# Attention on one core: the inner sums of V's blocks made by Pool instead of VectorE from the second batch on

## The chip, the cores and the metric

The kernel runs on one core of a Trainium2 chip. The metric is the device time of one execution in microseconds; runs of this kernel are compared by their medians. The core has five engines with instruction streams of their own: TensorE (PE in the profile, with its weight loads as PEld), VectorE (DVE), ScalarE (ACT), Pool (POOL) and SyncE (SP). Pool also issues most of this kernel's loads, so its stream is the queue of the loads as well.

## The reference

For each of 8 batches, with 2048 positions and a width of 512:

```python
scores = np.matmul(q, k.transpose(0, 2, 1)) / np.sqrt(d_k)
attn_weights = special.softmax(scores, axis=-1).astype(np.float32)
return np.matmul(attn_weights, v)
```

All three inputs and the output are float32 of 8 x 2048 x 512.

## The kernel before, in words

Both matrix products are made by a scheme that replaces the eight block products of a 2 x 2 by 2 x 2 product with seven, at the price of sums of blocks ahead of the products and behind them. Operands are float16, sums in PSUM are float32, the exponential is taken without subtracting a maximum, and the row sums of the weights come from a column of ones beside V.

**Scores.** A `Group` (L267 to L331) makes the scores of 1024 queries against 256 keys in seven products on PE (L299); ACT copies and exponentiates (L309, L313, L316, L239), DVE adds two products from PSUM into a buffer `cz` (L319, L322). The sums of K's and Q's blocks are made by DVE (L185 to L188, L202 to L205). The weights go into `left` and `right`.

**Weights times V.** There are 32 groups `g`, four to a batch, each with two blocks `a` and `b` of 256 rows of the output. `Pair` (L471) makes the products 1, 5, 6 and 7 (L512) of each block from the weights, V in `vh` and sums of V's blocks: `vt1`, `vt2` and `vt4`, made by DVE in L219 to L222, word `V` in the order below. The products 2, 3 and 4 of both blocks go through the same scheme once more, in `Leaf` (L402): seven inner products of three parts each (L424, 12 matmuls of 128 x 128), one part for each `h`. The inner V block of `h` = 0 is `vt4`, that of `h` = 1 and 2 the left and right half of the second rows of `vh`. DVE adds each inner product from PSUM into `rows` (L431), ACT scales the rows, and SP stores them.

**The sums that the change touches.** For each `h`, `leaf_v` (L364) cuts the inner V block into four quarters, and `leaf_v_sums` (L372) gives four subtractions on 128 x 512 float16 elements: `t1` and `t2` into buffers `vu` (L376, L377), the third over a quarter of the block itself (L378, it shows as `vh<-vh` or `vt<-vt`), `t4` into `vu` (L379). That is twelve a batch and 96 in all. The inner products read them: 5 reads `t1`, 6 reads `t2`, 7 the third, 4 reads `t4`; 1, 2 and 3 read the block's quarters as they are. There is one set of `vu` buffers for all batches, so a batch's `t1` may be written only when the last inner product 5 of the batch before has read the old one.

**What sets the order.** All engines' streams are written out by hand, as words in `SEQUENCES` (L620), one list for each of the four groups of a batch, with special ones at the start and at the end. Every engine works off its own instructions in that order; waits on semaphores are put in from the data's dependences. A word with a stroke belongs to the group before. The words of the change are `w`, `u` and `n` for `h` = 0, 1 and 2, with the number of the subtraction; `lq`, `lk` and `lv` load a quarter of the next batch's Q, K or V (L131, L211, issued by Pool), and `tq`, `tk` transpose it by a DMA that SP issues (L155). There are two buffers `stage` for the loads of Q and K, so each of these loads waits until the transpose of the load before last has landed. A stretch of the list of a batch's first group reads

```python
"b5 V30 . u0 lq1 . n2 tk0 a7 u1 . xb1 . n1 lv0 . . xa0 xb2 b1 . fa . ha xa1 u3 V31 "
```

The dots are products of the scores, the letters `a` and `b` products of `Pair`. The order is that of the text, but each engine goes through it at its own pace: Pool, which had only loads, ran far ahead of the others.

Of the kernel before, what the change touches and what calls it, by code (L numbers as in the profile page):

```python
# [12 lines left out]
def kernel(  # L13
# [21 lines left out]
    nc = tc.nc  # L35
# [142 lines left out]
    add, sub = nc.vector.tensor_add, nc.vector.tensor_sub  # L178
# [185 lines left out]
    def leaf_v(b, h):  # L364

        w = (vt4[:], vraw[b % 2][:, :, 1, 0:H], vraw[b % 2][:, :, 1, H:])[h]
        t1, t2, t4 = (t[:] for t in vus[h])
        b12 = w[:, 0:NK, Q:H]
        t3 = vraw[(b + 1) % 2][:, 0:NK, 0, h * Q:(h + 1) * Q] if b == B - 1 else b12
        return w[:, 0:NK, 0:Q], b12, w[:, NK:NJ, 0:Q], w[:, NK:NJ, Q:], t1, t2, t3, t4  # L370

    def leaf_v_sums(b, h):  # L372
        b11, b12, b21, b22, t1, t2, t3, t4 = leaf_v(b, h)
        b22, t1 = b22[:, :, 0:Q], t1[:, :, 0:Q]
        return [
            lambda: sub(t1, b12, b11),  # L376
            lambda: sub(t2, b22, t1),  # L377
            lambda: sub(t3, b22, b12),  # L378
            lambda: sub(t4, b21, t2),  # L379
        ]  # L380
# [317 lines left out]
    def step(g, word):  # L698
# [7 lines left out]
        if kind in "abL":  # L706
            pv(g, word)
        elif kind in "Klt":
            next_batch(g, word)
        elif kind == "k":  # L710
            k_sums(int(word[2]))[int(word[1])]()
        elif kind in "xyz":
            weight_sums(g, word)
        elif kind == "v":
            v_sums(g // NQT, int(word[2]))[int(word[1])]()
        elif kind == "V":
            v_sums(g // NQT, 2 * int(word[2]), 2)[int(word[1])]()
        elif kind == "q":
            sp = g // 2 + 1 + g % 2
            if sp < NP // 2:  # L720
                q_sums(sp)[int(word[1])]()
        elif kind in "wun":
            leaf_v_sums(g // NQT, "wun".index(kind))[int(word[1])]()
        elif kind in "fh":
            pairs[g, word[1]].add_right("fh".index(kind) + 1)
        elif kind == "S":
            if leafed(g):
                leaves[g].store(int(word[1]))
        elif kind == "s":
            if leafed(g):  # L730
                leaf_p_sums(g)[int(word[1])]()
# [165 lines left out]
```

## Time and profile before

| | |
|---|---|
| median of 2 runs | 783.42 us (783.31 to 783.54) |
| span of the profiled execution, first to last instruction | 781.0 us |
| what lies around the span, median less span | 2.4 us |
| PE busy | 774.9 us, 99% |
| DVE busy | 744.8 us, 95% |
| ACT busy | 632.4 us, 81% |
| POOL busy | 72.4 us, 9% |

The profile shows one execution. Its page gives the busy time of each engine, the chain of work that ended last, and groups of instructions by source line, with the number of them, the total, the mean of one and the idle time of the engine ahead of them. The trace behind it can be asked for the rows in order of time, for the waits, and for the busy time in chosen stretches. An instruction's duration on DVE reaches a little beyond the start of the next one, so the distance from start to start is shorter than the duration. The granted clock of PE is full (1.00) in all stretches looked at. Times in the text are from the start of the span. The batch shown as the example is the third; its sums lie between 228 and 262 us.

### The profile page before, as it was taken

The page shows a single profiled execution, that of the slowest core. Times are in us where ns is not written, and L with a number is a line of the kernel's source. Part 1 is how long each engine was busy: PE and PEld are TensorE (multiplying, and loading weights), DVE is VectorE, ACT ScalarE, POOL GpSimd, SP SyncE. Part 2 cuts the span into 40 slices and gives each one's busy share as a digit, 9 for nine tenths or more (in the row PEclk, how much of TensorE's full clock was granted, in tenths as well). Part 3 has the DMA queues.
Part 4 walks back from the last instruction along what each step waited for, and adds up shares of the span by engine and source line. Part 5 has one row for each costly group of instructions (what it writes and reads, how often), then busy time and mean ns, then how long its engine had stood idle before and what let it go on. Part 6 is the DMA issues. An engine that isn't in the chain of part 4 may idle for free.

```text
span 781.0 us, 17247 instructions
## 1 busy us (share of the span) xinstructions
PE 774.9 (99%) x6675; PEld 536.7 (69%) x6675; DVE 744.8 (95%) x1466; ACT 632.4 (81%) x1152; POOL 72.4 (9%) x106
## 2 busy tenths in 40 slices
PE   9999999999999999999999999999999999999997
PEld 6566776677766777667676676666776667766687
DVE  6899999999999999999999999999999999999996
ACT  5987888877888778887788877897779977898763
POOL 4011101001010010100100101001010011000000
PEclk9999999999999999999999999999999999999999
DMA  9999777959879696795977969779788995831023
GB/s 224 183 168 157 165 149 152 206 90 167 182 121 193 121 208 143 132 190 114 188 163 138 161 115 182 169 160 136 158 158 149 192 141 136 172 83 55 1 81 136
DMA packets 196386, 115.97 MB, mean 148 GB/s; under 512 B 122448, under 2 KB 187088, under 8 KB 196304
## 3 DMA queue, kind: packets, MB, share of 16 engines
q0 software_dynamic: 49664, 49.29, 41.4%
q1 hardware_dynamic: 145936, 64.73, 35.1%
q8 instruction: 52, 0.85, 0.4%
q10 hardware_dynamic: 704, 0.85, 0.3%
q14 instruction: 30, 0.25, 0.1%
HBM read 100.70 MB, written 33.55 MB: 172 GB/s over the span
## 4 chain that ended last, share of the span: by engine, by line
PE 98%; ACT 1%; DMA 0%; DVE 0%; issue 0%
PE t L299 48%; PE t L512 29%; PE t L424 19%; PE t L259 1%; PE t L165 1%; DMA rows<-in_q_dram 0%; ACT right L239 0%; ACT rows L444 0%; ACT t L309 0%; ACT left L239 0%; PE t L598 0%; ACT cz L316 0%; DVE stage L818 0%; DVE qraw L168 0%; DVE kraw L168 0%
## 5 line engine op out<-in xcount | busy, mean ns | idle before, releaser
L299 PE MATMUL t<-qraw,kraw 128*128 128x512 f16 x744 | 194.2, 379 | 0.0
L512 PEld LDWEIGHTS <-s 128*128 128x128 f16 x1536 | 148.2, 98 | 44.2 <-DVE s L353 0.3
L424 PEld LDWEIGHTS <-right 128*128 128x128 f16 x2232 | 138.1, 97 | 32.0 <-DVE right L397 0.4
L299 PEld LDWEIGHTS <-kraw 128*128 128x128 f16 x1008 | 95.9, 98 | 79.9 <-issue 0.4
L239 ACT ACTIVATE right<-cz 128x1024 f16<-128x1024 f32 x126 | 133.0, 1061 | 14.0 <-DVE cz L319 14.0
L299 PE MATMUL t<-qs,ks 128*128 128x512 f16 x504 | 138.7, 379 | 0.1
L512 PE MATMUL t<-vt,s 128*128 128x256 f16 (+1 forms) x1024 | 132.8, 273 | 0.0
L431 DVE TENSOR_TENSOR rows<-t,rows 128x384 f32<-128x384 f32 x217 | 119.2, 549 | 5.4 <-PE t L424 3.0
L299 PEld LDWEIGHTS <-ks 128*128 128x128 f16 x756 | 71.6, 98 | 58.3 <-issue 1.1
L239 ACT ACTIVATE left<-t 128x512 f16<-128x512 f32 x128 | 77.2, 603 | 25.9 <-PE t L299 23.5
L322 DVE TENSOR_TENSOR cz<-t,cz 128x512 f32<-128x512 f32 x126 | 86.3, 685 | 11.0 <-PE t L299 10.3
L239 ACT ACTIVATE right<-t 128x512 f16<-128x512 f32 x132 | 79.9, 607 | 11.6 <-PE t L299 8.5
L313 ACT COPY cz<-t 128x512 f32<-128x512 f32 x126 | 73.6, 584 | 18.2 <-PE t L299 15.5
L319 DVE TENSOR_TENSOR cz<-t,cz 128x512 f32<-128x512 f32 x126 | 86.0, 682 | 1.5 <-PE t L299 1.3
L444 ACT ACTIVATE rows<-rows,scales 128x512 f32<-128x512 f32 x124 | 83.0, 724 | 0.4 <-DVE rows L431 0.4
L316 ACT COPY cz<-t 128x512 f32<-128x512 f32 x126 | 74.9, 594 | 5.5 <-PE t L299 5.2
L309 ACT COPY t<-t 128x512 f32<-128x512 f32 x123 | 71.0, 577 | 6.8 <-PE t L299 2.0
L424 PE MATMUL t<-vh,right 128*128 128x128 f16 x1004 | 76.4, 218 | 0.0
L299 PE MATMUL t<-qraw,ks 128*128 128x512 f16 x252 | 75.0, 379 | 0.0
L299 PE MATMUL t<-qs,kraw 128*128 128x512 f16 x252 | 74.9, 379 | 0.0
L512 PE MATMUL t<-vh,s 128*128 128x256 f16 x512 | 66.4, 273 | 0.0
L512 PE MATMUL t<-vh,left 128*128 128x256 f16 x512 | 66.3, 273 | 0.0
(90 smaller groups left out, 979.2 us busy)
## 6 DMA issues: line engine op xcount, KB each, us to landing
out_dram<-rows SPq DMA_DIRECT2D x125, 256.0 KB, 2.9
vh<-in_v_dram POOLq DMA_DIRECT2D x32, 512.0 KB, 8.6
stage<-in_q_dram POOLq DMA_DIRECT2D x28, 512.0 KB, 5.9
stage<-in_k_dram POOLq DMA_DIRECT2D x28, 512.0 KB, 5.7
right<-in_k_dram POOLq DMA_DIRECT2D x2, 512.0 KB, 12.6
rows<-in_q_dram SPq DMA_DIRECT2D x2, 256.0 KB, 3.6
cz<-in_q_dram SPq DMA_DIRECT2D x2, 256.0 KB, 4.5
cz<-in_k_dram SPq DMA_DIRECT2D x2, 256.0 KB, 4.4
```

Of the source, the lines that this page charges most:

```text
L165: nc.tensor.transpose(tr[:, m, dc, :], src[:, n + m, dc * P:(dc + 1) * P], ident)
L239: nc.scalar.activation(out=out_, in_=in_, func=EXP, scale=inv_sqrt_d)
L299: nc.tensor.matmul(dst[:], lhs[:, j, dc, :], rhs[:, :, dc, :], start=(n in (1, 5) and dc == 0), stop=(dc == 1), skip_group_check=True,)
L309: self.edges[0](out=self.y[:], in_=self.x[:])
L313: self.edges[1](out=self.cz[:, 0, :], in_=self.z[:])
L316: nc.scalar.copy(out=self.cz[:, 1, :], in_=self.x[:])
L319: nc.vector.tensor_add(self.cz[:, 0, :], self.x[:], self.cz[:, 0, :])
L322: nc.vector.tensor_add(self.cz[:, 1, :], self.z[:], self.cz[:, 1, :])
L424: nc.tensor.matmul(to[:, h * Q:h * Q + w], lhs[:, j, h, :], rhs[:, j, 0:w], start=(n in (1, 2, 5) and h == 0 and j == 0), stop=(j == NK - ...
L431: nc.vector.tensor_add(o, part, o)
L444: nc.scalar.activation(out=o, in_=o, func=COPY, scale=scales[:, g % 2, m, 1 - h:2 - h])
L512: nc.tensor.matmul(dst[:, 0:width], lhs(j), rhs(j), start=(first and j == 0), stop=(j == NJ - 1), skip_group_check=True,)
```

## The change

One line is added to `leaf_v_sums`. For every batch but the first (`b` = 0) the four subtractions are given to Pool; in the first they stay on DVE. That moves 84 instructions from DVE's stream into Pool's. Their words, and so their places in the written order relative to the loads, stay the same.

```diff
@@ -372,6 +372,7 @@
     def leaf_v_sums(b, h):
         b11, b12, b21, b22, t1, t2, t3, t4 = leaf_v(b, h)
         b22, t1 = b22[:, :, 0:Q], t1[:, :, 0:Q]
+        sub = nc.gpsimd.tensor_sub if b else nc.vector.tensor_sub
         return [
             lambda: sub(t1, b12, b11),
             lambda: sub(t2, b22, t1),
             lambda: sub(t3, b22, b12),
             lambda: sub(t4, b21, t2),
         ]
```

Lines from 375 on have a number higher by one after the change.

On Pool, these rows stand in the third batch's first group and the start of its second before the change. `stage` rows are loads of Q and K, `vh` rows are loads of V; the number behind a name tells the buffer.

```order
L131 DMA stage_3126<-in_q_dram 128x4x512
L131 DMA stage_3134<-in_k_dram 128x4x512
L131 DMA stage_3239<-in_q_dram 128x4x512
L211 DMA vh1_94<-in_v_dram 128x4x512
L131 DMA stage_3308<-in_k_dram 128x4x512
L131 DMA stage_3482<-in_k_dram 128x4x512
```

The same place on Pool after the change (the first of the batch's twelve, which writes `vu1_2`, stands right ahead of the first row here):

```order
L131 DMA stage_3126<-in_q_dram 128x4x512
L131 DMA stage_3134<-in_k_dram 128x4x512
L377 TENSOR_TENSOR vu1_1_101<-vh0_93 128x512
L131 DMA stage_3239<-in_q_dram 128x4x512
L379 TENSOR_TENSOR vh0_93<-vh0_93 128x4x128
L378 TENSOR_TENSOR vu2_1_102<-vh0_93,vu1_1_101 128x512
L378 TENSOR_TENSOR vu2_2_105<-vh0_93,vu1_2_104 128x512
L211 DMA vh1_94<-in_v_dram 128x4x512
L380 TENSOR_TENSOR vu4_1_103<-vh0_93,vu2_1_102 128x512
L377 TENSOR_TENSOR vu1_0_98<-vt4_97 128x512
L131 DMA stage_3308<-in_k_dram 128x4x512
L380 TENSOR_TENSOR vu4_2_106<-vh0_93,vu2_2_105 128x512
```

Seven of the batch's twelve subtractions stand in these rows, and four more follow them ahead of the next load. Pool works in this order, so a load that stands behind a subtraction is issued after it, and a subtraction behind a load after that load's wait.

On DVE, these rows stand at the start of the batch's second group before the change. `s`, `left` and `right` are sums of the weights, `rows` and `cz` are fed from PSUM (`t`).

```order
L431 TENSOR_TENSOR rows0_115<-t_3396,rows0_115 128x3x128
L379 TENSOR_TENSOR vu4_2_106<-vh0_93,vu2_2_105 128x512
L397 TENSOR_TENSOR right0_109<-left0_107,right0_109 128x12x128
L378 TENSOR_TENSOR vh0_93<-vh0_93 128x4x128
L378 TENSOR_TENSOR vt4_97<-vt4_97 128x4x128
L377 TENSOR_TENSOR vu2_0_99<-vt4_97,vu1_0_98 128x512
L354 TENSOR_TENSOR s3_114<-left0_107,right0_109 128x1024
```

And the same place on DVE after the change:

```order
L432 TENSOR_TENSOR rows0_115<-t_3396,rows0_115 128x3x128
L398 TENSOR_TENSOR right0_109<-left0_107,right0_109 128x12x128
L354 TENSOR_TENSOR s3_114<-left0_107,right0_109 128x1024
L537 TENSOR_TENSOR rows0_115<-rows0_115 128x256
L322 TENSOR_TENSOR cz_3425<-t_3422,cz_3425 128x512
```

The four subtractions between are gone, and the sums of the weights and the additions from PSUM move up.

## Prediction

> **What bounds the kernel now.** I read the page first: busy times, then the chain that ended last.
>
> ```profile
> span 781.0 us, 17247 instructions
> PE 774.9 (99%) x6675; PEld 536.7 (69%) x6675; DVE 744.8 (95%) x1466; ACT 632.4 (81%) x1152; POOL 72.4 (9%) x106
> ...
> PE 98%; ACT 1%; DMA 0%; DVE 0%; issue 0%
> ```
>
> PE is the bound: 774.9 of 781.0 us, and 98% of the chain. So work taken from another engine can bring at most what PE idles, 6.1 us in the whole span. The sum is made against this execution's 781.0 us; the median of the runs, 783.42 us, is 2.4 us above it, and I add the sum to the median. DVE at 95% is close behind. Next I read the waits of the weight loads, where a late DVE would show first.
>
> ```profile
> PEld L424 <- DVE right L397: 0.4, 1, 0.4
> ...
> PEld L512 <- DVE s L353: 0.3, 1, 0.3
> ```
>
> These are the largest two behind the opening: PE hardly ever waits for DVE. Where DVE has room is seen by stretches of the third batch (columns: stretch, length, then busy time and count of PE, PEld, DVE, ACT, POOL).
>
> ```profile
> 211.00:228.00 17.00, 17.00 (x135) 11.08 (x134) 16.17 (x29) 15.12 (x29) 0.74 (x1) 1.00 0.86 156
> 228.00:245.00 17.00, 17.00 (x130) 11.11 (x129) 16.74 (x36) 15.92 (x31) 1.48 (x2) 1.00 0.90 186
> 245.00:262.00 17.00, 17.00 (x148) 11.86 (x147) 16.98 (x34) 13.16 (x24) 2.96 (x4) 1.00 0.94 133
> 262.00:286.00 24.00, 24.00 (x215) 16.91 (x214) 23.55 (x50) 17.64 (x34) 2.96 (x4) 1.00 0.79 159
> ```
>
> PE is full in all four. DVE is full as well exactly where the moved subtractions lie: 33.72 of 34 us in 228 to 262, which leaves 0.3 us. Time that DVE loses there is not taken from idle time, and PE is the next to feel it.
>
> **What is removed.** Twelve subtractions a batch, seven batches, 84 in all. Three of them follow each other on DVE:
>
> ```profile
> 256.79 0.41 DVE L378 TENSOR_TENSOR vh<-vh 128x512 f16<-128x512 f16 x1
> 257.13 0.41 DVE L378 TENSOR_TENSOR vt<-vt 128x512 f16<-128x512 f16 x1
> 257.46 0.41 DVE L377 TENSOR_TENSOR vu<-vt,vu 128x512 f16<-128x512 f16 x1
> 257.80 0.68 DVE L354 TENSOR_TENSOR s<-left,right 128x1024 f16<-128x1024 f16 x1
> ```
>
> One lasts 0.41 us but the next starts 0.34 us later, so a removed one frees 0.34 us: 12 x 0.34 = 4.1 us a batch, 28 us in all. By itself that brings nothing, since PE does not wait for DVE; the cover is PE's own work.
>
> **What is added on Pool: the price of one.** The trace has no subtraction on Pool. The nearest rows:
>
> ```profile
> L376 DVE TENSOR_TENSOR vu<-vh 128x512 f16<-128x512 f16 x16 | 6.6, 415 | 0.0
> L434 DVE TENSOR_TENSOR rows<-t,rows 128x1 f32<-128x1 f32 x62 | 9.1, 146 | 0.0
> L536 DVE TENSOR_TENSOR rows<-rows 128x256 f32<-128x256 f32 x62 | 25.8, 416 | 0.7
> L756 POOL MEMSET vu<- 128x4 f16 x1 | 0.1, 118 | 0.0
> L815 POOL CAST gate<-qraw 128x1 f32<-128x1 f16 x1 | 0.7, 693 | 21.8 <-DMA qraw<-right 21.8
> ```
>
> The low end is what DVE takes, 0.42 us. For the other ends I take an engine that gets through its operands one at a time. DVE passes one float32 element of both inputs in (416 - 146) / 255 = 1.06 ns; two inputs one behind the other are 2.12 ns, and 512 of them 1.08 us. With the 0.12 us of Pool's small memset that is 1.20 us, with the 0.69 us of its cast of one column 1.77 us. I take 1.20: the cast stood behind a wait, the memset is the plain small instruction. The range is 0.42 to 1.77.
>
> The Trainium skill (GPSIMD Engine Reference, Performance versus the Vector engine) gives 4497 ns for an addition of 2048 float32 elements on GpSimd against 2293 ns on VectorE; a quarter of it is an estimate of 1.12 us, with which the sum below would be 19 us instead of 23. No run here shows it yet.
>
> Beside its time on Pool, an operation that reads and writes the same memory can hold up DVE. The trace shows no case of it. The low end is none, the high end a DVE that stands still for the whole of each Pool operation. Between them I take that DVE is held while it would work on two inputs from SBUF, as Pool's subtraction does, and not while one input comes from PSUM. The PSUM rows of 228 to 262:
>
> ```profile
> L319 DVE TENSOR_TENSOR cz<-t,cz 128x512 f32<-128x512 f32 x7 | 4.8, 681 | 0.0
> L322 DVE TENSOR_TENSOR cz<-t,cz 128x512 f32<-128x512 f32 x6 | 4.1, 686 | 0.2 <-PE t L299 0.2
> L431 DVE TENSOR_TENSOR rows<-t,rows 128x384 f32<-128x384 f32 x7 | 3.8, 549 | 0.0
> ```
>
> 12.7 us of PSUM work, 4.1 us of moved work, and 33.7 - 12.7 - 4.1 = 16.9 us of other work from SBUF. Without the moved part that is 16.9 / 29.6 = 57%. So one Pool operation holds DVE for 0.57 x 1.20 = 0.68 us, twelve for 8.2 us. The end at none is 0; the other end is 12 x 1.77 = 21 us.
>
> The Trainium skill (SBUF — State Buffer, Who interferes with whom) says that GpSimd and a VectorE instruction with two SBUF inputs take turns on one read interface, whole instructions at a time, whichever starts first. Where two such instructions of DVE follow each other, that rule would hold DVE for the whole 1.20 us, which is the third rival below; no trace here shows it.
>
> **The sum.** DVE gains 4.1 us and loses 8.2 us in a stretch in which it has 0.3 us idle. How late may DVE be before PE waits? In order of time:
>
> ```profile
> 260.20 0.55 DVE L431 TENSOR_TENSOR rows<-t,rows 128x384 f32<-128x384 f32 x1
> ...
> 260.93 0.39 PE L424 MATMUL t<-vt,right 128*128 128x128 f16 x4
> ```
>
> This addition clears the PSUM bank at 260.75 and the next inner product into it starts at 260.93: 0.2 us. Another has more: the last `t2` starts at 257.46 above and ends at 257.87, its reader at 258.72 (below), 0.85 us. I allow 0.5 us. PE then loses 8.2 - 4.1 - 0.3 - 0.5 = 3.3 us a batch, and cannot win it back, since it is full everywhere. Seven batches make 23 us: 783.4 + 23 = 807 us (3.0% slower). With a Pool operation of 1.77 us the hold is 12.1 us a batch and the loss 50 us, 834 us. With 0.42 us the hold is 2.9 us, less than is freed, and the time stays.
>
> **The queue on Pool.** Pool ran ahead of the others, and its loads are late now:
>
> ```profile
> 208.17 0.74 POOL L131 DMA_DIRECT2D stage<-in_q_dram  x1 [18.58 <-DMA qraw<-stage]
> 218.72 0.74 POOL L131 DMA_DIRECT2D stage<-in_k_dram  x1 [9.80 <-DMA qraw<-stage]
> 230.96 0.74 POOL L131 DMA_DIRECT2D stage<-in_q_dram  x1 [11.50 <-DVE cz L322]
> ...
> 247.50 0.74 POOL L131 DMA_DIRECT2D stage<-in_k_dram  x1 [15.06 <-DMA kraw<-stage]
> ```
>
> The first subtraction of the batch may only start when the old `t1` has been read:
>
> ```profile
> 225.61 0.84 PE L424 MATMUL t<-vu,left 128*128 128x128 f16 x12
> ...
> 258.72 0.83 PE L424 MATMUL t<-vu,right 128*128 128x128 f16 x12
> ```
>
> That is 226.5 us, and the load of Q that went out at 208.17 stands behind it: 226.5 + 1.2 = 227.7, 19.5 us late. Landing and transpose, from the page's DMA rows and SP's rows:
>
> ```profile
> stage<-in_q_dram POOLq DMA_DIRECT2D x28, 512.0 KB, 5.9
> ...
> qraw<-stage SPq DMA_TRANSPOSE x28, 4.3
> ```
>
> ```profile
> 225.14 3.19 SPq L155 DMA_TRANSPOSE qraw<-stage  x1
> ...
> 243.25 3.21 SPq L155 DMA_TRANSPOSE qraw<-stage  x1
> ```
>
> It lands at 233.6 instead of waiting in its buffer, and its transpose goes out 8.5 us late and lands at about 237.9. The next load of Q, from 230.96, follows at 238.5, 7.5 us late, lands at 244.4, and its transpose is 1.1 us late. The stores behind these transposes on SP go out up to some microseconds later. The first reader of this Q:
>
> ```profile
> 269.78 0.68 DVE L202 TENSOR_TENSOR qs<-qraw 128x1024 f16<-128x1024 f16 x1
> ```
>
> It is 20 us away, so the late loads cost nothing. The subtractions behind the K load of 247.50 are tighter: that load is issued until 248.2, and four of them must be done before the inner product 6 at 258.72. Four at 1.2 us with a wait of about one DVE instruction each (0.6 us) take 7.2 us, to about 255.5: in time.
>
> **The rivals.**
> - *Not slower.* DVE is held for less than (4.1 + 0.3 + 0.5) / 12 = 0.41 us by each Pool operation, or not at all. Then what is freed covers it, PE stays full, and the time is 783 us. For it: nothing in the trace shows DVE lengthened by Pool's work, though that work is loads of 0.74 us, which take no operands from SBUF. Against it: DVE has no idle time just there, and most of its work reads the same memory. Chance 0.28.
> - *Pool's queue.* If a subtraction takes over (258.7 - 248.2) / 4 = 2.6 us with its wait for DVE, the inner product 6 waits for Pool, and each further 0.5 us costs four times that, 2 us a batch or 14 us: 797 us alone, 820 us on top of the forecast. Against it is that 2.6 us lies above both ends of the price. Chance 0.07.
> - *DVE stands still for the whole operation.* 12 x 1.20 = 14.4 us a batch, less 4.9 us, makes 9.5 us, 67 us in all: 850 us. Against it is the 12.7 us of PSUM work that lies between. Chance 0.09.
> - *Faster.* A DVE with 4 us more room a batch lets PE use its idle time. That is 6.1 us at most, most of it at the two ends of the span, and never 2%. Chance 0.01.
>
> **How the numbers follow.** The forecast, DVE held in part, has the remaining 0.55, and its own range is 791 to 834 us, from a hold of 0.5 us each (12 x 0.5 - 4.9 = 1.1 us a batch, 8 us) to the dear Pool operation. The range for 8 in 10 takes in *not slower* at its lower end, 782 us, and ends at 836 us. 2% of 783.4 is 15.7 us, about what a measurement of this kernel tells from no change; the border is 799 us, a hold of 0.6 us each. Of the forecast's 0.55 I put 0.10 below it; with *not slower* that makes 0.38 the same. *Pool's queue* and the whole hold are slower, as is the forecast's remaining 0.45: together 0.61. Faster is 0.01.
>
> **What would show it.** Right: rows of DVE with two SBUF inputs in 228 to 262 that last 1 us and more, or gaps ahead of them, while rows that read PSUM keep their 0.55 to 0.69 us; PE with waits on DVE of 3 us a batch, in the stretches of the twelve subtractions and not elsewhere; Pool rows of 1.2 us or more. The first load behind the batch's first subtraction should go out some 19 us later in the batch, with the Q sums not waiting for it. Wrong: DVE rows as before, with idle time of 4 us a batch, and PE full; or PE waiting for `vu` from Pool at L425, which would be the queue.

## The result, and the profile after

| | before | after |
|---|---|---|
| median of 2 runs | 783.42 us | 824.36 us (823.11 to 825.60) |
| span of the profiled execution | 781.0 us | 823.8 us |
| DVE busy | 744.8 us | 778.1 us |
| mean granted clock of PE in that execution | 1.000 | 0.987 |

The ratio is 1.0523, with a 95% interval of 1.0485 to 1.0561: 41 us slower. The forecast was 807 us, with a range of 782 to 836 us. The ratios here and below leave out, as slow, a run that lies over 1.5% above the fastest of its kernel; that is one run, of 803.32 us, with writes on Pool. The page after, with the engines' busy times and the chain:

```profile
span 823.8 us, 17277 instructions
PE 789.9 (96%) x6675; PEld 540.4 (66%) x6675; DVE 778.1 (94%) x1382; ACT 634.6 (77%) x1152; POOL 183.5 (22%) x190
...
PE 78%; DVE 18%; issue 3%; ACT 0%; DVEq 0%
```

DVE has 84 instructions fewer and is busy 33 us longer. PE's idle time went from 6.1 to 33.9 us, and 18% of the chain that ended last now runs through DVE, where it was nothing. The groups of DVE's rows (count | busy us, mean ns of one | idle time ahead), the first three with two inputs from SBUF, the last two with one from PSUM:

```profile
L354 DVE TENSOR_TENSOR s<-left,right 128x1024 f16<-128x1024 f16 (+3 forms) x80 | 60.3, 753 | 0.2
L397 DVE TENSOR_TENSOR left<-right 128x1536 f16<-128x1536 f16 x31 | 35.6, 1149 | 0.0
L535 DVE TENSOR_TENSOR rows<-rows 128x256 f32<-128x256 f32 x62 | 32.0, 516 | 0.0
...
L432 DVE TENSOR_TENSOR rows<-t,rows 128x384 f32<-128x384 f32 x217 | 119.8, 552 | 8.9 <-PE t L425 5.9
L322 DVE TENSOR_TENSOR cz<-t,cz 128x512 f32<-128x512 f32 x126 | 86.5, 686 | 15.0 <-PE t L299 13.9
```

The first of them before the change:

```profile
L354 DVE TENSOR_TENSOR s<-left,right 128x1024 f16<-128x1024 f16 (+3 forms) x80 | 45.8, 573 | 0.2
```

The additions from PSUM take what they took (549 and 685 ns before); the sums of the weights and the additions in `rows` have become longer (573, 947 and 414 ns before). So DVE is held, and only where both of its inputs come from SBUF. How, the rows in order of time show, in the second batch:

```profile
158.12 0.79 POOL L131 DMA_DIRECT2D stage<-in_k_dram  x1 [5.35 <-PE t L299]
158.45 0.55 DVE L432 TENSOR_TENSOR rows<-t,rows 128x384 f32<-128x384 f32 x1
158.92 5.21 DVE L397 TENSOR_TENSOR left<-right 128x1536 f16<-128x1536 f16 x1
158.92 1.06 POOL L380 TENSOR_TENSOR vu<-vh,vu 128x512 f16<-128x512 f16 x1
159.94 1.16 POOL L379 TENSOR_TENSOR vh<-vh 128x512 f16<-128x512 f16 x1
161.05 1.15 POOL L379 TENSOR_TENSOR vt<-vt 128x512 f16<-128x512 f16 x1
162.17 1.14 POOL L378 TENSOR_TENSOR vu<-vt,vu 128x512 f16<-128x512 f16 x1
163.39 1.75 POOL L380 TENSOR_TENSOR vu<-vt,vu 128x512 f16<-128x512 f16 x1
164.05 1.63 DVE L355 TENSOR_TENSOR right<-right,s 128x1024 f16<-128x1024 f16 x1
165.61 0.95 DVE L399 TENSOR_TENSOR right<-right 128x1536 f16<-128x1536 f16 x1
166.47 0.68 DVE L322 TENSOR_TENSOR cz<-t,cz 128x512 f32<-128x512 f32 x1
...
167.21 1.87 PE L299 MATMUL t<-qs,ks 128*128 128x512 f16 x4 [4.49 <-DVE cz L322]
```

Four subtractions stand back to back on Pool, and one DVE sum of 0.95 us lasts 5.21 us: it ends 0.82 us after the fourth. The fifth reads the fourth's result; its row is 1.75 us long, 0.7 us more than the first, and DVE gets in there. PE then waits 4.49 us for an addition that was queued behind the held sum. Such a row of four does not form in every batch. In the fourth the load of K ahead of it had not waited, and one of the subtractions had to wait for DVE, which parts them:

```profile
354.99 0.79 POOL L131 DMA_DIRECT2D stage<-in_k_dram  x1
...
361.47 1.47 POOL L379 TENSOR_TENSOR vt<-vt 128x512 f16<-128x512 f16 x1 [3.17 <-DVE vt L222]
```

The other hold of this length in this execution, 5.08 us at 569.99, again stands behind a load of K that had waited, for 9.23 us. The waits of PE in the whole trace:

```profile
PE t L299 <- DVE cz L322: 7.8, 4, 4.5
PE t L299 <- DVE cz L319: 6.8, 6, 1.6
PE t L513 <- DVE s L354: 4.6, 4, 2.5
PE t L425 <- DVE vt L222: 3.1, 2, 2.1
PE t L425 <- DVE right L398: 2.4, 1, 2.4
...
PE t L425 <- POOL vu L378: 0.5, 1, 0.5
```

Nearly all are for DVE; the one for a `vu` from Pool is 0.5 us. And after the long wait PE itself is slow (columns as before: length, busy times of PE, PEld, DVE, ACT, POOL, then the granted clock, the DMA engines' share and GB/s):

```profile
160.00:167.00 7.00, 2.72 (x27) 1.97 (x26) 7.00 (x4) 1.99 (x4) 5.06 (x4) 0.99 1.30 121
167.00:171.00 4.00, 3.79 (x15) 1.90 (x15) 3.62 (x7) 2.79 (x5) 0.79 (x1) 0.60 0.63 130
171.00:176.00 5.00, 5.00 (x55) 3.58 (x53) 4.36 (x9) 3.43 (x6) 0.62 (x1) 1.00 0.78 123
```

From 167 to 171 us the mean granted clock is 0.60, after which it is 1.00 again. Over the whole span the mean is 0.987, that is 0.013 x 823.8 = 10.7 us of lost clock. This is an upper end, since a slow clock costs nothing while PE idles.

### The profile page after: what moved, and what is told of

Same layout as the page of the kernel before. It is cut to its first block, busy times and chain, and to the rows that moved or that the text cites. A ratio compares the mean times of both kernels' runs of the same rounds, so it can differ in the third digit from the quotient of the medians.

```text
span 823.8 us, 17277 instructions
## 1 busy us (share of the span) xinstructions
PE 789.9 (96%) x6675; PEld 540.4 (66%) x6675; DVE 778.1 (94%) x1382; ACT 634.6 (77%) x1152; POOL 183.5 (22%) x190
## 4 chain that ended last, share of the span: by engine, by line
PE 78%; DVE 18%; issue 3%; ACT 0%; DVEq 0%
PE t L299 38%; PE t L513 22%; PE t L425 16%; DVE s L353 2%; DVE cz L319 2%; DVE s L352 2%; DVE cz L322 2%; DVE s L354 1%; DVE rows L535 1%; DVE rows L432 1%; DVE rows L537 1%; PE t L259 1%; PE t L165 1%; DVE right L355 1%; DVE left L397 1%
## 5 line engine op out<-in xcount | busy, mean ns | idle before, releaser
L299 PEld LDWEIGHTS <-kraw 128*128 128x128 f16 x1008 | 96.2, 98 | 90.9 <-issue 13.3
L299 PE MATMUL t<-qs,ks 128*128 128x512 f16 x504 | 141.4, 385 | 8.2 <-DVE cz L322 7.8
L377 POOL TENSOR_TENSOR vu<-vh 128x512 f16<-128x512 f16 x14 | 19.6, 1403 | 270.9 <-PE t L425 270.9
```

What stands on the lines that cost most here:

```text
L299: nc.tensor.matmul(dst[:], lhs[:, j, dc, :], rhs[:, :, dc, :], start=(n in (1, 5) and dc == 0), stop=(dc == 1), skip_group_check=True,)
```

## The experiments

Two theories went in. Theory 1: Pool's reads hold DVE, and the time freed on DVE is worth nothing, because PE was full. Theory 2: the loss comes from Pool's stream, in which loads now wait behind subtractions and subtractions behind loads. In all these kernels only the batches from the second on are touched. Lines of the edited kernels are shifted by some numbers. The time of before beside these runs was 783.3 to 783.5 us.

**The subtractions left out.**

```diff
+        if b:
+            return [lambda: None] * 4
```

> The twelve subtractions a batch are left out from the second batch on, on both engines, so the output is not attention; DVE is relieved by 4.1 us a batch and Pool has only its loads. Theory 1 (Pool's reads hold DVE, and what is freed on DVE is worth nothing): 783 us, within 1 us of before, because PE was full already. Theory 2 (the loss comes from Pool's stream: subtractions late, loads late behind them): also 783 us. If the time falls by more than 3 us, DVE's freed time has a worth of its own and both sums have to be corrected by it.

783.23 us, ratio 0.9999 (0.9990 to 1.0009). DVE without the sums:

```profile
PE 775.7 (99%) x6675; PEld 538.0 (69%) x6675; DVE 722.2 (92%) x1382; ACT 633.8 (81%) x1152; POOL 71.9 (9%) x106
```

DVE is busy 22.6 us less, and nothing comes of it. So, with the rest of the order as it is, no way of moving these sums elsewhere can beat the kernel before. Against this run the change's DVE is busy 778.1 - 722.2 = 55.9 us longer: 0.67 us of hold for each of the 84 Pool operations.

**The same places and waits, but narrow.** Each Pool subtraction is cut to `[:, :, 0:8]`, 32 of 512 elements.

```diff
+                lambda: ps(t1[:, :, 0:n], b12[:, :, 0:n], b11[:, :, 0:n]),
```

> The 84 subtractions stand on Pool at the same places and with the same waits, but each works on 32 of the 512 elements; the other 480 are left out. Theory 1: the hold goes with the length of the Pool operation; at some 0.2 us each, 2 us a batch against 4.1 us freed, no loss: 783 to 786 us. Theory 2: the order of Pool's stream and all its waits are those of the change, so most of the loss stays: over 805 us.

785.37 us (782.79 to 793.99 in 11 runs), ratio 1.0018 (1.0004 to 1.0033). The bulk of the loss goes with the length of the operation, as in theory 1, though shorter operations also make Pool's stream less late; the runs with writes below tell the two apart. Single runs are up to 10 us longer, which no hold explains, since DVE is busy for 722.9 us in the longest of them, 0.7 us more than without the sums.

**Half the length.** As above with 256 elements.

```diff
-            n = 8
+            n = 64
```

> As the change, but each Pool subtraction works on 256 of the 512 elements and the other half is left out. Theory 1: about 0.6 us each on Pool and half of the measured hold of 0.73 us, 12 x 0.37 = 4.4 us a batch against 4.1 us freed: 784 to 792 us. Theory 2: over 805 us, since order and waits are unchanged.

793.88 us (790.85 to 797.41), ratio 1.0137 (1.0096 to 1.0178). Just above what theory 1 gave, far below theory 2. (The 0.73 us of the expectation took 28 us as freed; with the 22.6 us measured above it is 0.67.) DVE is busy 740.6 us, 18.4 us more than without the sums, 0.22 us for each operation, and still less than before the change; a loss of 10 us does not follow from that. PE waits 3.7 us for DVE in the profiled execution, and 3.6 us for a `vu` from Pool.

**Writes instead of reads.** Pool writes a constant over the same elements.

```diff
+                lambda: ms(t1, 1.0),
```

> In place of the 84 subtractions Pool writes a constant over the same 512 elements, so the sums are left out and Pool reads nothing from SBUF; order and the waits for free places stay. Theory 1, with the reads as what collides: DVE rows with two SBUF inputs keep their times of before beside Pool's writes, 783 to 785 us. Theory 1 with any Pool access colliding: those DVE rows grow by the length of the write, and the time is over 785 us if that is 0.5 us or more. Theory 2: over 800 us.

789.46 us (788.79 to 797.07 in three runs), ratio 1.0109 (1.0056 to 1.0161). DVE is busy 722.0 us, as without the sums: writes hold nothing. Yet over 5 us are lost in each run. In the profiled execution, of 788.79 us, a clock of 0.998 takes up to 1.6 us of that, and the rest is in the main one wait of PE:

```profile
PE t L432 <- POOL vu L379: 4.0, 1, 4.0
```

It lies in the sixth batch. Pool's rows there and, as a contrast, the K load of the fifth batch, in which PE did not wait; then SP's transposes of both:

```profile
446.38 0.74 POOL L131 DMA_DIRECT2D stage<-in_k_dram  x1 [12.18 <-DMA kraw<-stage]
```

```profile
546.42 0.74 POOL L131 DMA_DIRECT2D stage<-in_k_dram  x1 [18.22 <-DMA kraw<-stage]
547.15 0.54 POOL L381 MEMSET vu<- 128x512 f16 x1
547.61 0.54 POOL L380 MEMSET vh<- 128x512 f16 x1
548.08 0.54 POOL L380 MEMSET vt<- 128x512 f16 x1
548.54 0.54 POOL L379 MEMSET vu<- 128x512 f16 x1
```

```profile
430.38 4.62 SPq L155 DMA_TRANSPOSE kraw<-stage  x1
```

```profile
525.65 9.60 SPq L155 DMA_TRANSPOSE kraw<-stage  x1
535.34 10.17 SPq L155 DMA_TRANSPOSE qraw<-stage  x1
```

The transpose of K takes 9.60 us to issue instead of 4.62, the K load waits 18.2 us for it, and the operations behind that load, the fourth of which makes `t2`, come too late for the inner product 6. Theory 2 has a part after all: not the late load itself, but what it runs into.

**Loads ahead again.** From here on the batch's first Pool operation stands behind the loads of Q and K, and V's load ahead of the next three.

```diff
-e L6' q1' L5' . . q2' n0 . . L7' . e
+e L6' q1' L5' . . q2' . . L7' . e
...
-b5 V30 . u0 lq1 . n2 tk0 a7 u1 . xb1 . n1 lv0 . .
+b5 V30 . n0 u0 lq1 lv0 . n2 tk0 a7 u1 . xb1 . n1 . .
```

The change itself with this order:

> The change with all its work, but the batch's first subtraction stands behind the loads of Q and K instead of ahead of them, and V's load ahead of the next three subtractions; no result changes. Theory 1 (Pool's reads hold DVE, 0.67 us each): the hold does not depend on the loads' places, 808 to 822 us, at most some 10 us less than the change. Theory 2 (loads held behind the first subtraction, and what follows from it): 783 to 790 us.

815.83 us, ratio 1.0413 (1.0397 to 1.0428): in theory 1's range. But the hold does depend on the loads' places: DVE is busy 770.5 us here, 48.3 us more than without the sums or 0.58 us for each operation, where it was 0.67, and its longest row is 2.58 us instead of 5.21.

The writes with this order:

> Pool writes a constant in place of the subtractions, which are left out, with the loads ahead as in the kernel before. Theory 1: no reads, no hold, 783 to 785 us. Theory 2, that the 10 us which writes cost in the order of the change come from the held loads: also 783 to 785 us. If 790 us or more stay, the writes cost something by themselves or the five subtractions behind the K load are late whatever the first one does.

783.21 us, ratio 0.9997 (0.9987 to 1.0006). Nothing is left of what the writes cost.

The half subtractions with this order:

> Subtractions of 256 of the 512 elements on Pool, the other half left out, loads ahead. The hold was 0.22 us each in the order of the change, 2.6 us a batch against 4.1 us freed. Theory 1: 783 to 786 us. If the 10 us lost in the order of the change are the hold's after all, 790 us or more stay; if they are the held loads', they go.

785.52 us, ratio 1.0027 (1.0017 to 1.0037): 8.4 us of the 10.6 us are gone. DVE is busy 736.6 us, 0.17 us for each operation.

The change once more:

> The change itself once more, for its spread and for the granted clock of each run. Both theories: 821 to 828 us. Where the clock is lower the time should be longer by about the span times what the clock lacks: 4 to 5 us between runs with 0.987 and 0.993.

827.97 us (822.84 to 830.28), ratio 1.0544 (1.0505 to 1.0583). The four runs are 822.84, 826.42, 829.51 and 830.28 us at a granted clock of 0.994, 0.988, 0.986 and 0.981: the order agrees, but 0.013 x 826 = 10.7 us of clock stand against 7.4 us of time, so this working gives too much. The order of the loads is worth 8.5 to 12 us of the loss, part of which may be the longer hold, and 32 us are left with the loads ahead. Of those, the busy times and PE's waits for DVE in this order:

```profile
PE 785.4 (97%) x6675; PEld 538.9 (66%) x6675; DVE 770.5 (95%) x1382; ACT 634.6 (78%) x1152; POOL 193.1 (24%) x190
```

```profile
PE t L425 <- DVE vt L222: 12.2, 6, 2.2
PE t L299 <- DVE cz L319: 6.2, 6, 1.2
```

PE idles 813.2 - 785.4 = 27.8 us, 21.7 us more than before, or 3.1 us a batch, most of it for DVE and none for Pool; the granted clock of 0.992 takes up to 0.008 x 813.2 = 6.5 us. The other 4 us stay open.

**One input instead of two.** Pool copies one of the inputs, loads ahead.

```diff
+                lambda: cp(out=t1, in_=b12),
```

> Loads ahead; in place of each subtraction Pool copies one of its inputs, 512 elements, so Pool reads one input instead of two and the sums are left out. Theory 1 (any Pool operation that reads SBUF holds DVE's rows with two SBUF inputs for as long as it lasts): those rows grow; with 0.5 to 0.7 us each on Pool the hold is like that of the half subtractions, 783 to 788 us. If only Pool's second input collides: rows as before and 783 us, as with the writes.

785.17 us, ratio 1.0026 (1.0016 to 1.0035). DVE is busy 735.3 us, 13.1 us more than without the sums, 0.16 us for each copy: one input of Pool is enough, and a copy, whose shortest row is 0.60 us, holds DVE as much as a half subtraction of 0.61 us. The lumps are here too. In the third batch five copies without a wait between them keep one addition of 0.41 us waiting:

```profile
248.41 3.30 DVE L542 TENSOR_TENSOR rows<-rows 128x256 f32<-128x256 f32 x1
```

The copies hold DVE for 1.9 us a batch, less than the 3.2 us freed (22.6 / 7), and still 1.9 us are lost: a lump costs time even where DVE gains on the whole.

**Which load it is.** Only the first Pool operation moved behind the loads of Q and K:

> Pool's writes in place of the subtractions, which are left out; only the batch's first one is moved behind the loads of Q and K, V's load stays behind the next three. Theory 2 with the held loads of Q and K as the cause of the 10 us: 783 to 785 us. With V's load as the cause: 790 to 797 us.

783.19 us, ratio 0.9998 (0.9989 to 1.0007). Only V's load moved ahead of the next three:

> Pool's writes in place of the subtractions, which are left out; only V's load is moved ahead of the next three, the first write stays ahead of the loads of Q and K. Theory 2 with the held loads of Q and K as the cause: 788 to 800 us as before the move. With V's load as the cause: 783 to 785 us.

783.16 us (782.55 to 788.54), ratio 1.0005 (0.9991 to 1.0019). Either move alone removes nearly all of it, so neither load alone is the cause: it takes the loads of Q and K behind the first operation and the late load of V together. One run of ten is still 5 us longer with the second. Both runs have writes in place of the subtractions; with the subtractions only both moves together were run.

**A late Pool without a hold.** The write that the inner product 6 reads first is made 24 times over.

```diff
-                lambda: ms(t2, 1.0),
+                lambda: [ms(t2, 1.0) for _ in range(1 if h else 24)],
```

> Loads ahead and Pool's writes in place of the subtractions, which are left out; the write that the inner product 6 reads first is made 24 times over, so that PE waits some 2.7 us for Pool in each of seven batches while DVE is not held. If PE loses the waits alone: 783 + 7 x 2.7 = 802 us at a granted clock of 1.00. If a wait of this length also brings 3.4 us at half clock each time, 1.7 us more each: about 814 us at a clock of 0.985.

803.54 us, ratio 1.0260 (1.0233 to 1.0287), at clocks of 0.991 to 0.995. PE waits six times for Pool, 14.5 us in all, which alone would give 798 us; the clock of the profiled execution, 0.993, takes up to 5.6 us more. It drops after two of the six waits. The rows of the two longest waits, and the clock around them:

```profile
266.29 1.44 PE L432 MATMUL t<-vu,right 128*128 128x128 f16 x12 [4.87 <-POOL vu L379]
...
562.57 0.83 PE L432 MATMUL t<-vu,right 128*128 128x128 f16 x12 [2.99 <-POOL vu L379]
```

```profile
264.00:271.00 7.00, 4.71 (x37) 3.61 (x37) 1.85 (x4) 1.53 (x2) 4.70 (x8) 0.53 0.45 59
563.00:570.00 7.00, 7.00 (x70) 4.79 (x68) 6.32 (x13) 4.15 (x7) 2.15 (x3) 1.00 0.87 124
```

After 4.87 us of waiting the clock is 0.53 and the same twelve matmuls take 1.44 us; after 2.99 us it is 1.00 and they take 0.83 us. The other drop follows a shorter wait, of 2.16 us to 365.81: from 366.11 to 369.52 the clock is 0.50. The result lies between the two expectations: a slow clock comes with PE's waiting, without DVE being held, but not after each wait, and not by the wait's length alone.

## Why the prediction was right, and where it was not

- **PE is the bound, and what DVE is relieved of is worth nothing: right.** With the sums left out the time is 783.23 us.
- **One Pool subtraction costs 1.20 us: nearly right.** The shortest rows are 1.04 us, as the view by line gives for `vu` from `vh` (min, median, max), and longer rows contain a wait for DVE:

```profile
L378 POOL TENSOR_TENSOR vu<-vh,vu x14: 1037/1048/1581, 147.4 to 748.7; 128x512 f16<-128x512 f16 x14
L378 POOL TENSOR_TENSOR vu<-vt,vu x7: 1138/1332/1862, 162.2 to 767.7; 128x512 f16<-128x512 f16 x7
```

  Between 32 elements (0.23 us at the shortest) and 512 an element takes (1.04 - 0.23) / 480 = 1.7 ns, where 2.12 was worked out from DVE's rows.
- **DVE is held for 0.68 us by each, in rows with two SBUF inputs and not in those from PSUM: right as to the rows, and by luck in part as to the size.** It is 0.67 us in the change. But 57% of the length, as the prediction had it, would be 0.35 us for a half subtraction and 0.34 us for a copy, and 0.22 and 0.16 us were measured; with the loads ahead even the whole one holds DVE for 0.58 us only. The Trainium skill (SBUF — State Buffer, Who interferes with whom) says that such rows contend with a GpSimd instruction that reads SBUF, and not with one that only writes it; the trace agrees in both, with 722.0 us of DVE beside Pool's writes against 722.2 us without.
- **Between two Pool operations DVE gets one instruction in, 0.6 us: wrong.** The step counted one such wait for each Pool operation. Four in a row without a wait between them made one DVE sum last 5.21 us. Here the rival *DVE stands still for the whole operation*, with its chance of 0.09, is what the rows show; on the mean it does not hold, since 0.67 us is about half of an operation. The sum of the hold is as forecast, but it comes in lumps, and a lump of 4 us passes any margin of 0.2 to 0.85 us.
- **PE loses 3.3 us a batch: right for the idle time.** It is 3.1 us with the loads ahead and 27.8 / 7 = 4.0 us in the change. The sum took DVE's whole debt against its margin; the copies above lose time without a debt, so that the two agree is in part luck.
- **"The late loads cost nothing": wrong.** The times at which they go out were right. All of the third batch lies 8.6 us later here (the last reader of the old `t1` starts at 234.19 instead of 225.61); less that, Q's loads went out at 228.1 and 238.7, where 227.7 and 238.5 were worked out:

```profile
234.19 0.84 PE L425 MATMUL t<-vu,left 128*128 128x128 f16 x12
...
236.70 0.79 POOL L131 DMA_DIRECT2D stage<-in_q_dram  x1
...
247.34 0.79 POOL L131 DMA_DIRECT2D stage<-in_q_dram  x1 [7.91 <-DMA qraw<-stage]
...
262.02 0.79 POOL L131 DMA_DIRECT2D stage<-in_k_dram  x1 [6.08 <-PE t L299]
```

```profile
248.14 6.60 SPq L155 DMA_TRANSPOSE kraw<-stage  x1
255.00 6.43 SPq L155 DMA_TRANSPOSE qraw<-stage  x1
```

  What failed is that the transposes kept their times of before: the one of K takes 6.60 us to issue where it took 3.73. By the trace it lands 13.3 us after its start, where it was 7.5 us. The K load behind it goes out at 262.02, 0.5 us after that landing, as before the change (so it is this that it waits for, though its row names PE), less the shift 5.9 us later than before, and the last five subtractions with it. The sum lacked 8.5 to 12 us for the order of the loads. That the stretched transposes come from loads and stores that now fall together on the DMA engines is argued from the rows; what is shown is that with writes moving either load takes the cost away. With the subtractions the cost comes another way than with the writes: PE waits 0.5 us for a `vu` from Pool, but a late K load can leave the subtractions behind it nothing to wait for, and both holds of over 5 us stand behind such loads. How much of the 8.5 to 12 us goes this way is not shown.
- **The clock: not in the sum.** It takes up to 10.7 us of the profiled execution's span. The other run of the change, at 0.994, should by this working be 5.8 us shorter and is 2.5 us shorter.

The sum was 23 us and the measured loss 41 us. By the profile the span grew by 42.8 us, 27.8 us of it PE's idle time and up to 10.7 us the clock; at least 4 us more lie in PE's busy time and stay open. That 824 us still lies in the range is luck in part: the range reaches so high for a Pool operation of 1.77 us, and nothing that made the loss larger than 23 us was in it. *Pool's queue*, a rival with a chance of 0.07 alone, took a part of the loss by another way than the one given there: it asks for 2.6 us for a subtraction with its wait, where the mean row is 1.3 us and the longest 2.42, but the load in front of them was late.

## What to carry to other kernels

Count what a moved instruction takes from its new neighbours before what it frees on the old engine: here 0.67 us of DVE lost for 0.27 to 0.34 us freed, with PE full and DVE 99% busy at that place. An in-order engine that issues loads far ahead of the rest stops doing so as soon as one instruction that waits for the others is put into its stream (here a load of Q went out some 20 us later); place such an instruction behind the loads it need not precede. Look at the longest single hold and not only at the sum: four subtractions in a row without a wait held DVE for the whole row, which no margin here could take. And try the removal first: a run with the work left out showed at once that no better place for it in this order could bring anything.

## What was not expected of the hardware

Consecutive Pool subtractions kept a DVE instruction with two SBUF inputs waiting through four of them, 5.21 us for a sum of 0.95 us, and let it in ahead of the fifth, which had to wait for the fourth's result.

After a wait PE can run at a low clock for some microseconds: 0.53 over 7 us after a wait of 4.87 us and 0.50 over 3.4 us after one of 2.16 us, but full clock after one of 2.99 us in the same execution. The Trainium skill (TensorE: Matmul & The Clock Gate, Part 1: The HAM clock gate) gives half rate after at least one idle window of about 3.4 us, with a window that runs freely; the waits of 4.87 and 2.99 us here agree with it, the one of 2.16 us does not. Nor does the change with the loads ahead: no wait of PE there is longer than 2.2 us, and its mean clock is 0.992, with 0.50 from 258.07 to 261.48 after a wait of 2.22 us. What decides after the shorter waits is not shown.
